# Mixer B's q, k and v of two head groups projected together, 512 columns wide, with roots taken on GpSimd

## The chip, the cores and the metric

The kernel runs on one core of one Trainium2 chip. The metric is the device time of one execution in microseconds (us). The core has a matmul engine (TensorE, PE), a vector engine (VectorE, DVE), an activation engine (ScalarE, ACT), a general engine (GpSimd, POOL) and a queue engine that only issues transfers here (SyncE, SP). Each works through its own instructions in order and waits for the others by semaphores.

## What is computed

The reference is a two-layer encoder trunk over 1024 tokens of width 1024. Layer 0 uses mixer A, a neighbourhood attention; layer 1 uses mixer B, which is what the change touches:

```python
def mixer_b(h, w_in, q_norm_g, k_norm_g, w_out):     # 16 query heads, 4 key/value heads, 64 wide
    proj = h @ w_in
    q, k, v, gate = jnp.split(proj, [MIX_WIDTH, MIX_WIDTH + kv_w, MIX_WIDTH + 2 * kv_w], axis=-1)
    q = rms_norm(q.reshape(b, s, B_Q_HEADS, HEAD_DIM), q_norm_g).transpose(0, 2, 1, 3)
    k = rms_norm(k.reshape(b, s, B_KV_HEADS, HEAD_DIM), k_norm_g).transpose(0, 2, 1, 3)
    v = v.reshape(b, s, B_KV_HEADS, HEAD_DIM).transpose(0, 2, 1, 3)
    q, k = _apply_axial_rope(q, tabs), _apply_axial_rope(k, tabs)
    ...
        sc = jnp.einsum('bkgqd,bksd->bkgqs', qb, k).astype(jnp.float32) * scale
        pr = jax.nn.softmax(sc, axis=-1).astype(v.dtype)
        return jnp.einsum('bkgqs,bksd->bkgqd', pr, v)
    ...
    return (o * jax.nn.silu(gate)) @ w_out
```

After each mixer come a residual sum, a per-layer gated embedding (the dense phase), and at the end a norm. Everything is in 32-bit floats.

## The kernel before

Tokens lie in 8 tiles of 128. The normalised input is kept transposed as a high and a low part, `HTh` and `HTl`, and each weight unit (128 x 1024) is split into a high part `wh` and a low part `wl`. A product is three matmuls, high x high, high x low, low x high (`split3`, through `mm`, so that nearly every matmul carries the line of `mm`). A weight unit is loaded by SyncE into `wstage`, ScalarE makes the high part and VectorE the low part (`Weights.pump`); the queue `q` sets the order of units, four slots hold units with slot number 1, and units with slot number 3 use a spare pair of the `KA`, `KB` buffers.

Mixer B has 4 groups of 4 query heads; a group shares one key/value head. The weights `bq` (256 columns of q for a group) and `bkv` (128 columns of k and 128 of v for a pair of groups) are applied by `q_items` and `kv_items`: for each token tile 8 x 3 matmuls of 256 columns into PSUM, cut into two pieces of 12 by `proj_N`, after which ScalarE copies the result out and squares it for the RMS norm, and two pieces of work later (`post.add(DR, rot)`) the sums and the rotation follow (`rope_in`). After every fourth tile `finish_norm` computes the inverse roots of the sums (`rsqrt_ops`: a bit-level first guess and three Newton steps, 11 small VectorE operations) and GpSimd multiplies them in (`scale_tile`). `k_stack` and `q_stack` then transpose k and q on TensorE into the layout of the scores. Gates (`gate_items`) are matmuls of 512 columns, in pieces of six.

The prologue, before attention starts, is written out by hand as the list `pre`: k, v of pair 0, q of group 0, the two halves of the k stack among the q pieces, the first query stack, the gate of pair 0 and the first scores. Between its first pieces it also transposes what is still pending from the dense phase (`pend`, `to_ht`): six pieces, of which the first two lie in buffers of the dense phase (`xn`). The first tiles of the prologue use the two score buffers of PSUM (`psS`).

Attention takes 32 steps per group: a step's scores (`f_S`), VectorE's minimum, ScalarE's exponential, transposes (`f_T`), and products with V. `mix` hands out the other, dense pieces between the steps in proportion: for group 0 the q of group 1 and a gate, for group 1 two gates, k, v of pair 1 and q of group 2, for group 2 two gates and q of group 3, for group 3 gate and embedding products. In the dense pieces of groups 0 to 2 the rotation runs on GpSimd.

Mixer A contains 32 transfers issued by GpSimd that add into DRAM (`weight_sums`); those are the only ones whose descriptors GpSimd writes, into a scratch at the start of SBUF that the program reserves (16 KB per partition unless it says otherwise).

## Time and profile before

| what | value |
|---|---|
| time, median of 3 runs | 1502.16 us (1500.39 to 1502.37) |
| profiled execution, its own time | 1500.79 us |
| its span in the trace | 1499.0 us |
| granted TensorE clock, mean | 0.998 of full speed |
| busy in the span: PE, DVE, ACT, POOL | 1478.6, 1069.6, 916.3, 445.2 us |
| mixer B's prologue | 694.6 to 757.2 us |
| groups 0, 1, 2 (by their first minimum on VectorE) | 757.2, 882.2, 1042.1 to 1178.2 us |

The span runs from the first to the last instruction in the trace; the own time has 1.8 us around it. Times inside the trace are counted from the span's start. "Busy" adds up the times in which an engine has an instruction running; matmuls overlap each other, so the rate of matmuls is read from their starts, not from their durations.

### The profile page before, as it was taken

How to read it: one execution, taken by the hardware profiler on the slowest of the kernel's cores; microseconds unless marked ns; L12 is line 12 of the kernel's file. 1: busy time of each engine (PE TensorE's matmuls, PEld its weight loads, DVE VectorE, ACT ScalarE, POOL GpSimd, SP SyncE). 2: the span in 40 equal slices, each digit the busy share in tenths (PEclk: the TensorE clock that was granted, in tenths of full speed). 3: DMA queues.
4: the chain of work that ended last, by engine and by line, in shares of the span. 5: the costliest groups of instructions: out<-in, count | busy, mean ns of one | idle time of the engine just before them, and what ended most of it. 6: DMA issues, size and time to landing. Idle time of an engine off the chain costs nothing.

```text
span 1499.0 us, 24720 instructions
## 1 busy us (share of the span) xinstructions
PE 1478.6 (99%) x8881; PEld 1302.8 (87%) x8881; DVE 1069.6 (71%) x2027; ACT 916.3 (61%) x1860; POOL 445.2 (30%) x637
## 2 busy tenths in 40 slices
PE   8999999999999999999999999999999999999997
PEld 8888988988988888888988999989999988888886
DVE  6666476477477598756887786777877787789845
ACT  6676476477477535433567776666767777745432
POOL 3355475387265200020322122443130300000000
PEclk9999999999999999999999999999999999999999
DMA  8424374283132862262210111111111122763223
GB/s 263 140 93 127 81 167 138 64 171 97 36 89 85 328 247 99 92 207 80 77 50 22 33 48 42 47 33 43 59 28 48 38 78 64 246 234 108 79 98 128
DMA packets 91466, 157.70 MB, mean 105 GB/s; under 512 B 18256, under 2 KB 54352, under 8 KB 90832
## 3 DMA queue, kind: packets, MB, share of 16 engines
q1 hardware_dynamic: 87344, 143.80, 28.9%
q0 software_dynamic: 2560, 8.39, 3.7%
q10 hardware_dynamic: 1440, 3.94, 0.8%
q8 instruction: 71, 1.16, 0.3%
q14 instruction: 51, 0.42, 0.1%
HBM read 125.56 MB, written 50.83 MB: 118 GB/s over the span
## 4 chain that ended last, share of the span: by engine, by line
PE 86%; DVE 6%; DMA 3%; ACT 2%; issue 1%; POOL 1%; SPq 1%; DVEq 0%; POOLq 0%; ACTq 0%
PE d L322 53%; PE s L322 11%; PE o L322 11%; PE t L1329 7%; PE t L821 2%; PE t L504 2%; DMA HTl<-yD0l 1%; DMA X<-in_x 1%; DVE wl L236 1%; PE t L322 1%; DVE PTl L1332 1%; DVE mn L1311 0%; PE t L1281 0%; DMA ppD<-G 0%; DVE xn L1674 0%
## 5 line engine op out<-in xcount | busy, mean ns | idle before, releaser
L322 PE MATMUL d<-wh,HTh 128*128 128x256 f32 (+1 forms) x1000 | 330.7, 335 | 0.3 <-ACT G L654 0.2
L322 PE MATMUL d<-wh,HTl 128*128 128x256 f32 (+1 forms) x1000 | 326.8, 331 | 0.5 <-DVE HTl L506 0.5
L322 PE MATMUL d<-wl,HTh 128*128 128x256 f32 (+1 forms) x1000 | 325.9, 330 | 0.6 <-DVE wl L1461 0.6
L1332 DVE TENSOR_TENSOR PTl<-t,PTh 128x512 fp32r<-128x512 f32 x256 | 164.6, 685 | 104.5 <-ACT PTh L1331 104.2
L322 PEld LDWEIGHTS d<-wl,HTh 128*128 128x128 f32 x1000 | 187.6, 189 | 20.2 <-DVE wl L1461 1.0
L322 PEld LDWEIGHTS d<-wh,HTh 128*128 128x128 f32 x1000 | 187.4, 189 | 19.9 <-ACT G L654 0.5
L322 PE MATMUL d<-HTh,wh 128*128 128x512 f32 x504 | 204.6, 406 | 0.0
L322 PEld LDWEIGHTS d<-wh,HTl 128*128 128x128 f32 x1000 | 187.5, 189 | 19.1 <-DVE HTl L506 0.9
L322 PE MATMUL d<-HTh,wl 128*128 128x512 f32 x504 | 198.1, 393 | 0.0
L322 PE MATMUL d<-HTl,wh 128*128 128x512 f32 x504 | 197.3, 392 | 0.0
L1317 ACT ACTIVATE P<-s,mn 128x1024 f32<-128x1024 f32 x128 | 142.9, 1117 | 47.9 <-DVE mn L1311 46.9
L1331 ACT ACTIVATE PTh<-t 128x512 fp32r<-128x512 f32 x256 | 139.4, 594 | 45.7 <-PE t L1329 45.2
L1311 DVE TENSOR_REDUCE mn<-s 128x1 f32<-128x1024 f32 x128 | 155.0, 1211 | 9.7 <-PE s L322 9.2
L831 POOL TENSOR_TENSOR PTh<-PTh,SIDE 128x256 fp32r<-128x256 f32 x96 | 81.4, 848 | 194.2 <-ACT PTh L826 194.1
L1329 PE MATMUL t<-ident,P 128*128 128x128 f32 x1024 | 134.9, 273 | 2.6 <-DVE PTl L1332 2.0
L322 PE MATMUL s<-KA,QS 128*128 128x512 f32 (+2 forms) x384 | 134.0, 403 | 0.0
L1329 PEld LDWEIGHTS t<-ident,P 128*128 128x128 f32 x1024 | 115.3, 140 | 12.9 <-DVE PTl L1332 7.1
L322 PE MATMUL s<-KB,QS 128*128 128x512 f32 (+2 forms) x384 | 121.5, 370 | 0.0
L322 PE MATMUL o<-PTl,V 128*128 128x256 f32 (+2 forms) x672 | 120.2, 290 | 1.1 <-DVE PTl L1332 0.6
L322 PE MATMUL o<-PTh,V 128*128 128x256 f32 (+2 forms) x672 | 118.3, 287 | 2.6 <-POOL PTh L831 1.3
L236 DVE TENSOR_TENSOR wl<-wstage,wh 128x1024 fp32r<-128x1024 f32 x79 | 98.1, 1243 | 29.3 <-ACT wh L231 29.0
L322 PEld LDWEIGHTS d<-HTh,wl 128*128 128x128 f32 x504 | 94.6, 188 | 21.6
(272 smaller groups left out, 2860.9 us busy)
## 6 DMA issues: line engine op xcount, KB each, us to landing
wstage<-in_wts SPq DMA_DIRECT2D x88, 512.0 KB
pp<-ppD SPq DMA_DIRECT2D x32, 256.0 KB
X<-in_x SPq DMA_DIRECT2D x15, 512.0 KB
rb<-rD SPq DMA_DIRECT2D x58, 128.0 KB
ppD<-th SPq DMA_DIRECT2D x20, 256.0 KB
tD0t<-in_wts SPq DMA_DIRECT2D x16, 256.0 KB
tD1t<-in_wts SPq DMA_DIRECT2D x16, 256.0 KB
xD<-X SPq DMA_DIRECT2D x8, 512.0 KB
```

The source lines that it names most:

```text
L236: eng.tensor_tensor(lo[:, c:c + n], s[:, c:c + n], hi[:, c:c + n], ALU.subtract)
L322: pe.matmul(ps, a, b, start=first, stop=last, skip_group_check=True)
L504: pe.transpose(ps[:, k], xn[:, (4 * c + k) * 128:(4 * c + k + 1) * 128], ident)
L821: pe.transpose(ps[:, i], sp[:, c * 128:(c + 1) * 128], ident)
L831: pool.tensor_tensor(pt[:, 3 * j - 1:3 * j + 4:4], pt[:, f1:f1 + 1].to_broadcast([128, 2, 128]), SIDE[:, :2], ALU.mult)
L1311: dve.tensor_reduce(mn, ps, axis=AX.X, op=ALU.min)
L1317: act.activation(p, ps, AF.Exp, bias=mn, scale=-1.0, accum_out=RS[h, hf][:, t:t + 1])
L1329: pe.transpose(ps[:, i], p[:, k * 128:(k + 1) * 128], ident)
L1331: act.activation(PTh[:, ks, c], ps, AF.Copy)
L1332: dve.tensor_tensor(PTl[:, ks, c], ps, PTh[:, ks, c], ALU.subtract)
```

## The change

The weight layout gets units `bqkv`: for group 0 with pair 0, and for group 1 with pair 1, the 256 columns of q and the 128 of k and 128 of v stand side by side, so that four units replace two of `bq` and two of `bkv`. `qkv_items` replaces `kv_items` and the first two uses of `q_items`: 8 x 3 matmuls of 512 columns for each tile, in two pieces of 12. ScalarE copies all 512 columns out and squares 384 of them. q of group 1 and k, v of pair 1 are computed together (`second`): the first two tiles at the end of the prologue, the other six beside group 0's attention; group 1 keeps the stacks of the second pair, two gates and q of group 2. The gates move: group 0 has gate 1, group 1 gates 2 and 3, group 2 gates 4 and 5, group 3 gates 6 and 7. The prologue becomes: eight wide tiles, with one half of the k stack after the sixth and the first query stack after the seventh, the gate of pair 0 (its weight in the spare `KA`, `KB` pair), the other half of the k stack after six of that gate's eight pieces, then the first two tiles of the second projection among the first scores. Pending transposes are taken before every piece from the second on, not before every other one from the third on.

Outside the prologue the roots are computed by one VectorE operation, GpSimd's power with exponent -0.5 (in columns of 16), and one Newton step of three VectorE operations; in the prologue they stay as they were, and k is scaled by VectorE there, q by GpSimd. The buffers `qtp`, `vp` and `tab` get more copies, and the scratch for software DMA is 2 KB instead of 16 KB.

```diff
@@ lay_out
-    for i in range(4):
+    for i in range(2, 4):
         put([("bq", i, 0), ("bq", i, 1)], bq[:, i * 256:(i + 1) * 256], 4)
     for i in range(2):
         s = slice(i * 128, (i + 1) * 128)
-        put([("bkv", i, 0), ("bkv", i, 1)], np.concatenate([bk[:, s], bv[:, s]], axis=1), 4)
+        put([("bqkv", i, u) for u in range(4)],
+            np.concatenate([bq[:, i * 256:(i + 1) * 256], bk[:, s], bv[:, s]], axis=1), 2)
@@ order of the weight units
-    q += [(("bkv", 0, 0), 1), (("bkv", 0, 1), 1), (("bq", 0, 0), 1), (("bq", 0, 1), 1), (("bg", 0), 1)]
-    for gi in range(4):
-        if gi > 0:
-            q.append((("bg", 2 * gi), 1))
-        if gi == 1:
-            q += [(("bkv", 1, u), 1) for u in range(2)]
+    for i in range(2):
+        q += [(("bqkv", i, u), 1) for u in range(4)] + [(("bg", i), 3)]
+    for gi in range(1, 4):
+        q.append((("bg", 2 * gi), 1))
         if gi < 3:
             q += [(("bq", gi + 1, u), 1) for u in range(2)]
         q.append((("bg", 2 * gi + 1), 1))
@@ proj_N
-            def end(k1=k1):
+            def end(k0=k0, k1=k1):
+                if release:
+                    WQ.done(*[u for u in release if k0 <= (keys.index(u) + 1) * per - 1 < k1])
                 if k1 == nk:
-                    if release:
-                        WQ.done(*release)
                     leave(lambda: evac(st["ps"]))
@@ mixer_b
-            qtp = es.enter_context(tc.tile_pool(name="qtp", bufs=3))
-            vp = es.enter_context(tc.tile_pool(name="vp", bufs=3))
+            qtp = es.enter_context(tc.tile_pool(name="qtp", bufs=5))
+            vp = es.enter_context(tc.tile_pool(name="vp", bufs=4))
...
-                tab = sb.tile([128, 2, 64], F32, name="tab", bufs=2)
+                tab = sb.tile([128, 2, 64], F32, name="tab", bufs=4)
@@ finish_norm
+                if pro[0]:
+                    ops = [lambda: dve.tensor_scalar(ss, ss, 0.5 / HD, 0.5 * EPS, op0=ALU.mult, op1=ALU.add)]
+                    ops += rsqrt_ops(ss, ss, wk)
+                    for i in range(2):
+                        post.add(1 + i, lambda i=i: [f() for f in ops[6 * i:6 * i + 6]])
+                    for raw, rs in tiles:
+                        post.add(2, lambda raw=raw, rs=rs: scale_tile(raw, rs, dve if rs.shape[1] == 2 else pool))
+                    return
+                y, a = wk[:, 0:n], wk[:, n:2 * n]
+
+                def power():
+                    dve.tensor_scalar(ss, ss, 4.0 / HD, 4.0 * EPS, op0=ALU.mult, op1=ALU.add)
+                    for c in range(0, n, 16):
+                        w = slice(c, min(c + 16, n))
+                        pool.tensor_tensor(y[:, w], ss[:, w], mhalf[:, :w.stop - c], ALU.pow)
+
+                def newton():
+                    dve.tensor_tensor(a, y, y, ALU.mult)
+                    dve.scalar_tensor_tensor(a, a, -1.0, ss, op0=ALU.mult, op1=ALU.mult)
+                    dve.scalar_tensor_tensor(ss, a, 3.0, y, op0=ALU.add, op1=ALU.mult)
+                post.add(DR, power)
+                post.add(DR + NP - 1, newton)
+                for i, (raw, rs) in enumerate(tiles):
+                    post.add(DR + NP + i, lambda raw=raw, rs=rs: scale_tile(raw, rs))
@@ qkv_items, in place of kv_items
+            def qkv_items(i, eng):
+                keys = [("bqkv", i, u) for u in range(4)]
...
+                    def evac(ps, t=t):
...
+                        raw = sb.tile([128, 512], F32, name="th")
+                        act.activation(raw, ps, AF.Copy)
+                        red = sumsq(raw[:, :384], 6, ss[:, t])
...
+                        def rot():
+                            red()
+                            rope_in(kr, raw[:, 256:384], tabk, eng)
+                            rope_in(qt, raw[:, :256], tabq, eng)
+                            for v, c in vs:
+                                eng.tensor_tensor(v[:, 64:], c, v[:, :64], ALU.subtract)
+                        post.add(1 if pro[0] else DR, rot)
...
+                    items += proj_N(keys, t, 512, alloc, evac, release=keys if t == NT - 1 else (), kstep=4)
@@ the prologue
-            pre = kv[:-2] + qi[:6] + kv[-2:-1] + qi[6:10] + kv[-1:] + qi[10:14]
-            fill = qi[14:] + [d for hf in range(2) for d in gate_items("bg", 0, hf, dalloc, sb, gg)]
-            pre += [glue(lambda: q_stack(0, 0))] + fill[:5]
-            pre += [glue(lambda: f_S(*steps[0]))] + fill[5:6] + [glue(lambda: f_E(*steps[0]))] + fill[6:7]
-            pre += [glue(lambda: f_S(*steps[1]))] + fill[7:]
+            first, second = qkv_items(0, dve), qkv_items(1, pool)
+            ks, gf = stacks(0), gates(0)
+            pre = first[:12] + ks[:1] + first[12:14] + [glue(lambda: q_stack(0, 0))] + first[14:]
+            pre += gf[:6] + ks[1:] + gf[6:] + second[:2]
+            pre += [glue(lambda: f_S(*steps[0]))] + second[2:3] + [glue(lambda: f_E(*steps[0]))]
+            pre += [glue(lambda: f_S(*steps[1]))] + second[3:4]
             for i, d in enumerate(pre):
-                if i >= 2 and i % 2 == 0 and pend:
+                if i >= 1 and pend:
                     to_ht(psT, *pend.pop(0))
@@ dense pieces of the groups
-                if g > 0:
-                    dense += left
-                if g < 3:
-                    qi = q_items(g + 1, pool)
-                    kv = kv_items(1, pool) if g == 1 else [None, None]
-                    dense += kv[:-2] + qi[:KS] + [k for k in kv[-2:-1] if k] + qi[KS:8] + [k for k in kv[-1:] if k] + gates(2 * g + 1) + qi[8:]
-                    left = gates(2 * g + 2)
+                if g == 0:
+                    gd = gates(1)
+                    n = len(gd) // 2
+                    dense += second[4:8] + gd[:n] + second[8:] + gd[n:]
...
+                else:
+                    gd = gates(2 * g)
+                    n = len(gd) // 2
+                    qi = q_items(g + 1, pool)
+                    ks = stacks(1) if g == 1 else []
+                    dense += gd[:n] + ks[:1] + gd[n:] + qi[:KS] + ks[1:] + qi[KS:8] + gates(2 * g + 1) + qi[8:]
@@ kernel
-    nc = bacc.Bacc("TRN2", target_bir_lowering=False, num_devices=1)
+    nc = bacc.Bacc("TRN2", target_bir_lowering=False, num_devices=1, dynamic_dma_scratch_size=2048)
```

What the change moves is shown at three places. First ScalarE at the start of mixer B, where the last copies of the transposed input (`HTh<-t`, from `to_ht`) stand among the copies of the first projection tiles out of PSUM (`th<-s`), before the change:

```order
L505 ACTIVATE HTh_75<-t_7468 128x512
L1834 ACTIVATE wstage_7476,sq_6706<-X7_6048 128x512
L1249 ACTIVATE th_7557<-s_7524 128x256
L1157 ACTIVATE t1_7559<-th_7557 128x128
L1255 ACTIVATE V_7550<-th_7557 128x64
L1255 ACTIVATE V_7553<-th_7557 128x64
L505 ACTIVATE HTh_75<-t_7563 128x512
L1249 ACTIVATE th_7605<-s_7572 128x256
```

And the same place with the change:

```order
L1863 ACTIVATE wstage_7476,sq_6706<-X7_6048 128x512
L504 ACTIVATE HTh_75<-t_7539 128x512
L1269 ACTIVATE th_7563<-s_7526 128x512
L1156 ACTIVATE t1_7565<-th_7563 128x384
L1275 ACTIVATE V_7559<-th_7563 128x64
L1275 ACTIVATE V_7560<-th_7563 128x64
L504 ACTIVATE HTh_75<-t_7582 128x512
L504 ACTIVATE HTh_75<-t_7606 128x512
L1269 ACTIVATE th_7625<-s_7593 128x512
```

One copy of transposed input has moved ahead of the first tile, and two instead of one stand between the first two tiles; the copy and the squares are wider.

Second VectorE in the prologue, after the last tile whose k the second half of the k stack transposes: the end of the roots (`ss`, `wk`) and what follows, with `wl1` the low half of a weight unit, before the change:

```order
L339 TENSOR_TENSOR wk_7912<-wk_7912 128x8
L340 TENSOR_TENSOR wk_7912<-wk_7912,ss_7556 128x8
L341 SCALAR_TENSOR_TENSOR ss_7556<-wk_7912 128x8
L1158 TENSOR_REDUCE ss_7963<-t1_7965 128x4
L1145 TENSOR_TENSOR t2_7992<-qt_7962,tab_7916 128x8x16 x2
L1146 TENSOR_TENSOR qt_7962<-qt_7962,tab_7916 128x256
L1148 TENSOR_TENSOR qt_7962<-qt_7962,t2_7992 128x256
```

And with the change:

```order
L338 TENSOR_TENSOR wk_8006<-wk_8006 128x24
L339 TENSOR_TENSOR wk_8006<-wk_8006,ss_7561 128x24
L340 SCALAR_TENSOR_TENSOR ss_7561<-wk_8006 128x24
L1193 TENSOR_TENSOR qt_7558<-qt_7558,ss_7561 128x128 x4
L627 SCALAR_TENSOR_TENSOR G_8074<-th_8073,G_8074 128x512
L237 TENSOR_TENSOR wl1_8092<-wstage_8063,wh1_8091 128x1024
L237 TENSOR_TENSOR wl1_8103<-wstage_8065,wh1_8102 128x1024
L1241 TENSOR_TENSOR KB_7887<-th_8099,KA_7886 64x512
```

The roots of k and q are now one set of 24 columns, VectorE scales k itself (`qt_7558` holds k), and the rotations of q no longer follow behind the k roots but stand before them, tile by tile.

Third GpSimd from the same place on, before the change:

```order
L1179 TENSOR_TENSOR qt_7549<-qt_7549,ss_7556 128x128 x8
L1227 COPY KA_7551<-KA_7551 64x512
L1228 COPY KB_7552<-KB_7552 64x512
L1227 COPY KA_7554<-KA_7554 64x512
L1179 TENSOR_TENSOR qt_7962<-qt_7962,ss_7963 128x256 x4
L1228 COPY KB_7555<-KB_7555 64x512
```

And with the change, from the scaling of q of tiles 4 to 7:

```order
L1193 TENSOR_TENSOR qt_7814<-qt_7814,ss_7561 128x256 x4
L1246 COPY KA_7886<-KA_7886 64x512
L1247 COPY KB_7887<-KB_7887 64x512
L1246 COPY KA_7888<-KA_7888 64x512
L1144 TENSOR_TENSOR t2_8175<-th_8167,tab_8130 128x4x16 x2
L1145 TENSOR_TENSOR qt_8162<-th_8167,tab_8130 128x128
L1147 TENSOR_TENSOR qt_8162<-qt_8162,t2_8175 128x128
L1144 TENSOR_TENSOR t2_8180<-th_8167,tab_8128 128x8x16 x2
L1145 TENSOR_TENSOR qt_8166<-th_8167,tab_8128 128x256
L1147 TENSOR_TENSOR qt_8166<-qt_8166,t2_8180 128x256
L1283 TENSOR_TENSOR V_8163<-th_8167,V_8163 128x64
L1283 TENSOR_TENSOR V_8164<-th_8167,V_8164 128x64
```

GpSimd no longer scales k in the prologue, and the rotation of the second projection's first tile, q, k and v from one copy `th`, now follows the copies of k directly.

## Rows read from the trace of the kernel before

**Rows 1.** The page's busy times: us, share of the span, instructions.
```profile
PE 1478.6 (99%) x8881; PEld 1302.8 (87%) x8881; DVE 1069.6 (71%) x2027; ACT 916.3 (61%) x1860; POOL 445.2 (30%) x637
```

**Rows 2.** Windows of prologue and groups: busy us by engine, then clock, DMA share, GB/s.
```profile
694.60:757.20 62.60, 61.41 (x467) 58.83 (x468) 52.00 (x165) 28.51 (x72) 12.61 (x21) 1.00 0.21 68
757.20:882.20 125.00, 124.68 (x882) 113.68 (x881) 97.03 (x147) 92.86 (x171) 29.65 (x43) 1.00 0.11 34
882.20:1042.10 159.90, 158.55 (x1132) 146.81 (x1131) 117.04 (x202) 109.05 (x216) 62.86 (x112) 1.00 0.15 44
1042.10:1178.20 136.10, 136.10 (x956) 126.00 (x955) 105.30 (x166) 97.59 (x179) 34.02 (x48) 1.00 0.14 41
```

**Rows 3.** Timeline of PE, 256 columns, first and last of 43: start, us.
```profile
716.07 0.28 PE L322 MATMUL s<-wh,HTh 128*128 128x256 f32 x1
...
721.11 0.28 PE L322 MATMUL s<-wh,HTh 128*128 128x256 f32 x1
```

**Rows 4.** Timeline of PE, 512 columns, first and last of 57.
```profile
544.64 0.39 PE L322 MATMUL d<-wh,HTh 128*128 128x512 f32 x1
...
557.43 0.39 PE L322 MATMUL d<-wh,HTl 128*128 128x512 f32 x1
```

**Rows 5.** Chain that ended last, merged: start, us; prologue piece and attention piece.
```profile
705.94 2.88 PE s L322 x24
...
805.01 1.39 PE d L322 x6
```

**Rows 6.** Chain at the start of the prologue, 701 to 703.
```profile
701.05 0.45 PE t L504 x4
```

**Rows 7.** Timeline of PE there; idle time and releaser in brackets.
```profile
702.36 0.39 PE L322 MATMUL s<-wh,HTh 128*128 128x256 f32 x1 [0.88 <-ACT th L1249]
```

**Rows 8.** Chain before the first query stack, 738 to 746.
```profile
741.20 2.07 POOL qt L1179 x3
```

**Rows 9.** Waits of PE, 694 to 1180: us in total, times, longest.
```profile
PE t L1281 <- POOL qt L1179: 0.3, 1, 0.3
```

**Rows 10.** Timeline of DVE in the prologue.
```profile
704.07 0.28 DVE L1158 TENSOR_REDUCE ss<-t 128x2 f32<-128x128 f32 x1
...
705.56 0.69 DVE L506 TENSOR_TENSOR HTl<-t,HTh 128x512 fp32r<-128x512 f32 x1
...
731.34 0.41 DVE L1158 TENSOR_REDUCE ss<-t 128x4 f32<-128x256 f32 x1
...
732.98 0.41 DVE L1158 TENSOR_REDUCE ss<-t 128x4 f32<-128x256 f32 x1
...
737.77 0.17 DVE L1165 TENSOR_SCALAR ss<-ss 128x16 f32<-128x16 f32 x1
...
740.07 0.69 DVE L1222 TENSOR_TENSOR KB<-th,KA 64x512 fp32r<-64x512 f32 x1
...
744.48 0.40 DVE L1158 TENSOR_REDUCE ss<-t 128x4 f32<-128x256 f32 x1
...
747.09 0.69 DVE L1222 TENSOR_TENSOR KB<-th,KA 64x512 fp32r<-64x512 f32 x1
...
749.76 1.41 DVE L1291 TENSOR_TENSOR QS<-th,QS 64x512 fp32r<-64x512 f32 x2
751.19 1.23 DVE L236 TENSOR_TENSOR wl<-wstage,wh 128x1024 fp32r<-128x1024 f32 x1
```

**Rows 11.** Lines of ACT by shape, 695 to 1320: busy, mean ns, idle before.
```profile
L623 ACT ACTIVATE G<-d 128x512 f32<-128x512 f32 x15 | 9.0, 599 | 13.5 <-PE d L322 13.5
```

**Rows 12.** Lines of POOL by shape, whole span.
```profile
L1145 POOL TENSOR_TENSOR t<-qt,tab 128x128 f32<-128x128 f32 x48 | 22.5, 490 | 164.2 <-ACT qt L1193 50.4 <-PE t L1329 46.4 <-issue 40.7
...
L346 POOL TENSOR_TENSOR wkn<-sa,mhalf 128x4 f32<-128x4 f32 x2 | 2.0, 1010 | 20.8 <-DVE sa L1659 20.8
```

**Rows 13.** Line 680, software DMA: ns min/median/max, first and last start.
```profile
L680 POOL DMA_DIRECT2D tD0t<-tD0t x8: 780/1200/1967, 185.3 to 207.0; - x8
...
DMA to landing us min/median/max: 3.7/5.0/6.9
```

More of the change, by code (lines that the diff above doesn't have):

```diff
@@ L64, in weight_units @@
     names += [("ag", p) for p in range(8)]
-    for g in range(4):
+    for i in range(2):
+        names += [("bqkv", i, u) for u in range(4)]
+    for g in range(2, 4):
         names += [("bq", g, u) for u in range(2)]
-    for i in range(2):
-        names += [("bkv", i, u) for u in range(2)]
     names += [("bg", p) for p in range(8)]
@@ L173, in trunk @@
     make_identity(nc, ident)
-    mhalf = glob.tile([128, 4], F32, name="mhalf")
+    mhalf = glob.tile([128, 16], F32, name="mhalf")
     pool.memset(mhalf, -0.5)
@@ L1124, in mixer_b @@
             gg, ylive = {}, {}
-            KA, KB, V, QT, QST, P, RS, OP = {}, {}, {}, {}, {}, {}, {}, {}
+            KA, KB, KR, V, QT, QST, P, RS, OP = {}, {}, {}, {}, {}, {}, {}, {}, {}
             later = Later()
@@ L1155, in sumsq @@
             def sumsq(ps, nh, ss):
-                t1 = sb.tile([128, 256], F32, name="t1", bufs=1)[:, :nh * 64]
+                t1 = sb.tile([128, 384], F32, name="t1", bufs=1)[:, :nh * 64]
                 act.activation(t1, ps, AF.Square)
@@ L1164, in finish_norm @@
                 wk = sb.tile([128, 96], F32, name="wk", bufs=1)
-                ops = [lambda: dve.tensor_scalar(ss, ss, 0.5 / HD, 0.5 * EPS, op0=ALU.mult, op1=ALU.add)]
-                ops += rsqrt_ops(ss, ss, wk)
-                per = -(-len(ops) // (2 if pro[0] else NP))
-                at = DR
-                for i in range(0, len(ops), per):
-                    post.add(at, lambda i=i: [f() for f in ops[i:i + per]])
-                    at += 1
-                for raw, rs in tiles:
-                    post.add(at, lambda raw=raw, rs=rs: scale_tile(raw, rs))
-                    at += 0 if pro[0] else 1
@@ L1176, in scale_tile @@
-            def scale_tile(raw, rs):
+                n = ss.shape[1]
+                if pro[0]:
+                    ops = [lambda: dve.tensor_scalar(ss, ss, 0.5 / HD, 0.5 * EPS, op0=ALU.mult, op1=ALU.add)]
+                    ops += rsqrt_ops(ss, ss, wk)
+                    for i in range(2):
+                        post.add(1 + i, lambda i=i: [f() for f in ops[6 * i:6 * i + 6]])
+                    for raw, rs in tiles:
+                        post.add(2, lambda raw=raw, rs=rs: scale_tile(raw, rs, dve if rs.shape[1] == 2 else pool))
+                    return
@@ L1208, in q_items, with k_stack @@
                 return items
-            def k_stack(i, raw, hf):
+            def k_stack(i, hf):
+                raw = KR[i]
+                if hf == 0:
+                    for j in range(2):
+                        KA[2 * i + j] = kp.tile([128, 1024], F32R, name="KA")
+                        KB[2 * i + j] = kp.tile([128, 1024], F32R, name="KB")
                 ps = psT.tile([128, 4, 128], F32, name="t")
@@ L1352, in mixer_b, with gates, stacks @@
             pro[0] = True
-            kv, qi = kv_items(0, dve), q_items(0, dve)
+            WQ.cap[3] = 1
             glue = lambda f: (f, 0.0)
-            pre = kv[:-2] + qi[:6] + kv[-2:-1] + qi[6:10] + kv[-1:] + qi[10:14]
-            fill = qi[14:] + [d for hf in range(2) for d in gate_items("bg", 0, hf, dalloc, sb, gg)]
-            pre += [glue(lambda: q_stack(0, 0))] + fill[:5]
-            pre += [glue(lambda: f_S(*steps[0]))] + fill[5:6] + [glue(lambda: f_E(*steps[0]))] + fill[6:7]
-            pre += [glue(lambda: f_S(*steps[1]))] + fill[7:]
+            def gates(p):
+                return [i for hf in range(2) for i in gate_items("bg", p, hf, dalloc, sb, gg)]
+            def stacks(i):
+                return [(lambda hf=hf: k_stack(i, hf), 450.0) for hf in range(2)]
+            first, second = qkv_items(0, dve), qkv_items(1, pool)
[4 more added lines that the diff above has]
+            pre += [glue(lambda: f_S(*steps[1]))] + second[3:4]
             for i, d in enumerate(pre):
-                if i >= 2 and i % 2 == 0 and pend:
+                if i >= 1 and pend:
                     to_ht(psT, *pend.pop(0))
```

45 lines of the change are left out of this document (18 added, 27 removed).

## The prediction

> **What bounds the kernel now.** I read the busy shares first: TensorE is busy for 99% of the span, VectorE for 71%, GpSimd for 30% [rows 1]. Then I cut mixer B into its prologue and its first three head groups. The reader is to see in the windows that TensorE is idle for only 1.19, 0.32, 1.35 and 0.00 us of them, at a granted clock of 1.00, that is at the 2.4 GHz level, throughout [rows 2]. So nearly all that can be won is TensorE's own work, and nearly all that can be lost is a new wait of TensorE. Neither the 71% nor the 30% limits anything by itself, but in the prologue VectorE is busy for 52.00 of 62.60 us, and there a late VectorE can hold TensorE.
>
> "Busy" hides the rate at which matmuls follow each other, so I read starts. 256-column matmuls follow at 0.120 us (43 starts, 716.07 to 721.11: 5.04 / 42) [rows 3]. 512-column ones follow at 0.228 us (57 starts, 544.64 to 557.43: 12.79 / 56) [rows 4]. Two narrow ones cost 0.240, a wide one 0.228, for the same columns.
>
> **The change, part by part.**
>
> *Wide instead of narrow matmuls.* The q projections of groups 0 and 1 and the k, v projections of both pairs are 4 x 192 = 768 matmuls of 256 columns; they become 384 of 512. I count in pieces of 12 wide ones for 24 narrow: 32 pieces, 20 in the prologue and 12 among group 0's attention steps. 24 narrow take 2.88 [rows 5]. 12 wide take 12 x 0.228 = 2.74 in a quiet stretch; between attention steps six took 1.39, so 12 take 2.78 [rows 5]. 20 x 0.14 + 12 x 0.10 = **4.0 us won**. Ends: all at 0.10, 3.2; all at 0.14, 4.5.
>
> The Trainium skill, "TensorE: Matmul & The Clock Gate", section "Back-to-back issue gap", gives N/2.4 ns plus 2.5 ns between isolated matmuls at the full clock. By that, 24 narrow and 12 wide take 2.62 and 2.59 us, and the 32 pieces would win an estimated 1.0 us, not 4.0: a rule that speaks against the change. The rows show 120 and 228 ns where it has 109 and 216, so each instruction here costs some 13 ns beside its columns, and I go by the rows.
>
> *The entry.* Before, TensorE stood for 0.88 at 702.36, for ScalarE's first copy out of PSUM [rows 7]. That copy stood on ScalarE behind the second of the two transposed pieces that still lay in the earlier stage's buffers (701.05, ended 701.50) [rows 6], while both score buffers were full. Now these two pieces stand before the second and third half tile instead of before the third and fifth, and filling the second buffer takes 2 x 2.74 us instead of 2.88. The copy is therefore done some 5 us before TensorE wants the buffer: **0.9 won** (ends 0 and 0.9).
>
> *The first query stack.* GpSimd scaled three tiles of q from 741.20 to 743.27 [rows 8], and TensorE waited 0.3 for it [rows 9]. Now tile 3 ends three wide tiles ahead of that stack (3 x 2 x 2.74 = 16 us), against some 10 us of work: 1.5, 3.1, 2.3 and 1.2 as worked out for the next step, and 4 x 0.69 of GpSimd's scales [rows 8]: **0.3 won** (ends 0 and 0.3).
>
> *The second k stack.* This is the new wait. Before, the k roots were ready long before q was projected, and nothing else stood behind them. Now k of tiles 4 to 7 is ready only after the last wide tile, and six gate pieces (6 x 1.39 = 8.3) lie between that tile and the transposes that need it. In that time: ScalarE's copy of 512 columns 0.60 [rows 11] and the squares, which I put at the same, with 0.3 of hand-overs, 1.5; VectorE's k part 1.49 (704.07 to 705.56) and q part 1.64 (731.34 to 732.98), together 3.1; eleven root operations 2.3 (737.77 to 740.07); a weight's low half between them 1.2; four k scales at an estimated 0.3 (the seven operations of the k part take 0.21 each), 1.2 [rows 10]. Sum 9.3. VectorE also comes about 0.5 late to that tile, because the stack's query halves (1.41) and another low half (1.23) stand in front [rows 10]. 9.3 + 0.5 - 8.3 = **1.5 lost**. Below: 0, if hand-overs and scales are shorter. Above: with GpSimd working beside it the q part took 2.61 (744.48 to 747.09) instead of 1.64 [rows 10]; if all 7.8 us of VectorE's chain stretch by a quarter, 3.5. Behind the waiting transposes stand all of TensorE's queue, so the wait counts in full.
>
> The Trainium skill, "SBUF — State Buffer", section "Who interferes with whom", says that VectorE with two SBUF inputs and a GpSimd instruction that reads SBUF exclude each other. By that rule, the trace agrees: 2.61 against 1.64. The upper end is the row's with or without it; GpSimd has only query scales and three short copies to do there.
>
> *Attention of groups 0 and 1.* The dense work beside their 32 steps was 34 us (16 x 1.44 for q and 8 x 1.39 for a gate) and 68 (32 x 1.44 and 16 x 1.39). It becomes 44 (12 x 2.78 and 8 x 1.39) and 45 (16 x 1.44 and 16 x 1.39), and 45 is what group 2 has. Group 2 has no idle time, groups 0 and 1 have 1.67 together [rows 2]. The stacks of the second pair stay in group 1, with their waits. I take **0.5 won**; ends 1.7 won, 1.5 lost, if GpSimd's longer rotations hold the two shared scratch tiles. GpSimd has ten operations of about 0.5 for a tile [rows 12], 5 us, and two pieces of dense work with the attention steps between them are longer than that; only at the start do two tiles follow closely, with copies of k between them.
>
> *Costed at nothing.* The roots by power: GpSimd's power took 1.01 for 4 columns [rows 12] and now has up to 24, at most 6 us; all of it lies in groups 0 to 2, where the stacks that need it stand a gate projection or more behind; if that cover went, those 6 us a set would show. Root work taken from VectorE (8 small operations a set): not on the path in attention. The four weight units are again the first four in the queue, so they are split where four were split before. The second pair's units are freed one by one at tile 7 and have some ten pieces of work until they are wanted. The table loads go from one to two per tile on SyncE's queue, each with two tiles of lead by four buffers; behind them there stand weight loads and row sums, which are fetched earlier than they are used by more than that. The smaller scratch: the transfers that use it are 32, issued by GpSimd in mixer A, at most two in flight at the times shown [rows 13].
>
> **Sum.** -4.0 - 0.9 - 0.3 + 1.5 - 0.5 = -4.2. The profiled execution took 1500.79 (span 1499.0 and 1.8 outside), so 1496.6 in its terms. The median of the runs, 1502.16, is 1.37 above it; on that footing **1498.0**. All good ends give -7.4, all bad ends +1.8.
>
> **Rivals.**
> - *No new wait, and even groups.* The k stack comes in time and groups 0 and 1 run like group 2: another 1.5 and 1.2 won, 1495.3. For it: group 2's windows. Against: VectorE's sum above. Chance 0.15.
> - *The new wait eats the gain.* Wide matmuls win only 3.2, the k stack waits 3.5 and attention gives nothing: -3.2 - 0.9 - 0.3 + 3.5 = -0.9, 1501.3. For it: VectorE's stretched rows. Chance 0.24.
> - *It does not do what it says:* a wide matmul takes as long as two narrow ones. Then -0.2, 1502.0. Rows 3 and 4 speak against it. Chance 0.03.
> - *Slower: the scratch throttles GpSimd.* The second eight transfers of a layer are issued 3.1 us apart (185.3 to 207.0, seven intervals) and land in 5.0 [rows 13]. If the small scratch held fewer than two, each would wait 1.9 for the one before: 16 x 1.9 = 30 us of GpSimd time in mixer A, where it edits the score tiles that TensorE reads. If a third of that came through, +10: 1508. It decides as soon as one transfer fills the scratch; nothing in the trace shows its size. Chance 0.08.
>
> The forecast itself has 0.50, and its own range is 1496 to 1499.5.
>
> **How the numbers follow.** 0.2% is 3.0 us, about what a measurement of this kernel can tell from no change: faster means under 1499.2, slower over 1505.2. Of the forecast's 0.50, 0.43 lies below 1499.2; with the first rival 0.58 faster. 0.07, 0.24 and 0.03 make 0.34 the same; 0.08 slower. The range 1494.5 to 1502.5 takes in everything but the slower rival and the outer edges of the others.
>
> **What would show it.** The 512-column projection matmuls start 0.228 apart in the prologue and no more than 0.232 between steps. No wait stands before the third tile's first matmul. TensorE's largest idle time in the prologue stands before the second k stack's transposes, 1 to 2 us, ended by VectorE's k scale. Groups 0 and 1 have about equal lengths, near 135 us. GpSimd's transfers take as long as before. I am wrong if the wide matmuls keep 0.24, if that wait is over 3.5, or if TensorE waits for GpSimd in group 0.

## The result, and the profile after

The changed kernel is slower: 1505.53 us in the median of 11 runs (1503.74 to 1508.0) against 1502.16 of the kernel before, ratio 1.0021 (95% interval 1.0013 to 1.0029). The forecast was 1498.0, and its range ended at 1502.5. The profiled execution took 1508.0, 7.2 more than that of before (1500.79).

The busy times of the page, as in [rows 1]:

```profile
PE 1478.2 (98%) x8497; PEld 1284.1 (85%) x8497; DVE 1060.0 (70%) x1933; ACT 911.4 (61%) x1828; POOL 461.2 (31%) x637
```

TensorE has 384 matmuls less and the same busy time, since a wide one counts longer. The loss is in idle time. The windows of prologue and groups 0, 1, 2, cut at each group's first minimum as in [rows 2]:

```profile
694.60:767.30 72.70, 68.95 (x312) 55.77 (x311) 52.85 (x148) 30.63 (x65) 11.54 (x19) 0.98 0.24 77
767.30:912.80 145.50, 139.11 (x846) 119.83 (x845) 102.26 (x143) 96.28 (x182) 63.53 (x105) 1.00 0.13 38
912.80:1051.50 138.70, 137.07 (x952) 125.20 (x951) 101.77 (x149) 99.43 (x182) 37.63 (x49) 1.00 0.11 31
1051.50:1186.20 134.70, 134.70 (x946) 124.97 (x945) 104.99 (x153) 98.70 (x180) 39.51 (x50) 1.00 0.15 46
```

The lengths can't be set against those of before one by one, since work has moved between the stages; the idle times can. They were 1.19, 0.32, 1.35 and 0.00; they are 3.75, 6.39, 1.63 and 0.00, so 8.9 more. And the granted clock of the prologue is 0.98 instead of 1.00. Who was waited for, first in the prologue, then in group 0 (us in total, times, longest; `PTh` and `PTl` are the high and low parts of the transposed probabilities `P`):

```profile
PE t L1232 <- DVE qt L1193: 2.2, 4, 1.4
PE t L503 <- DVE HTl L505: 1.3, 1, 1.3
...
PE t L1350 <- DVE PTl L1353: 2.8, 3, 1.3
PE o L321 <- ACT PTh L1352: 1.6, 6, 0.3
PE t L1302 <- DVE PTl L1353: 1.3, 1, 1.3
PE t L1350 <- ACT P L1338: 0.6, 3, 0.2
```

The first row is the second k stack, where the forecast had put its new wait. TensorE's timeline there (idle time and releaser in brackets):

```profile
752.11 0.39 PE L321 MATMUL o<-HTh,KB 128*128 128x512 f32 x1
753.93 0.30 PE L1232 MATMUL t<-ident,qt 128*128 128x128 f32 x1 [1.43 <-DVE qt L1193]
754.46 0.33 PE L1232 MATMUL t<-ident,qt 128*128 128x128 f32 x1 [0.23 <-DVE qt L1193]
755.08 0.39 PE L1232 MATMUL t<-ident,qt 128*128 128x128 f32 x1 [0.29 <-DVE qt L1193]
755.70 0.47 PE L1232 MATMUL t<-ident,qt 128*128 128x128 f32 x1 [0.23 <-DVE qt L1193]
755.83 0.77 PE L321 MATMUL o<-HTh,KA 128*128 128x512 f32 x1
756.40 0.63 PE L321 MATMUL o<-HTl,KA 128*128 128x512 f32 x1
...
758.53 0.44 PE L321 MATMUL o<-HTh,KA 128*128 128x512 f32 x1
758.81 0.39 PE L321 MATMUL o<-HTl,KA 128*128 128x512 f32 x1
```

Two things are to be seen. All four transposes wait, each for its own k scale. By starts the wait is 3.0: 755.70 - 752.11 is 3.59, of which a wide matmul (0.23) and three transposes (0.11 each) are work. And behind it 512-column matmuls follow at 0.43 instead of 0.23 until 758.5: 755.83 to 758.81 is 2.98 for seven, which take 1.59 at full rate, another 1.4 lost. The windows of 2 us there show the same as a mean granted clock of 0.55 and 0.59, that is for the most part the 1.2 GHz level:

```profile
753.00:755.00 2.00, 0.63 (x2) 1.00 0.73 215
755.00:757.00 2.00, 1.69 (x5) 0.55 0.34 113
757.00:759.00 2.00, 2.00 (x7) 0.59 0.16 23
759.00:761.00 2.00, 2.00 (x10) 1.00 0.98 279
```

What was forecast as won is there. The chain shows 72 wide matmuls of the prologue (six pieces) and one piece of group 0:

```profile
716.13 16.38 PE s L321 x72
...
857.20 2.73 PE d L321 x12
```

16.38 / 72 is 0.2275, and 2.73 / 12 the same.

Up to the end of group 2 the profiled execution is 8.0 later (1186.2 against 1178.2). That is about 8.9 of idle time, 1.4 of the slow clock and 2 for what the brackets leave out (the wait at 753.93 is 1.43 there and 1.59 by starts; some 14 gaps more at 0.15), less 4.5 of narrow matmuls saved (below), and 0.6 by which this execution came later to the projection's first matmul (695.16 against 694.60). Together 8.4. The medians differ by less, 3 to 5 us: the profiled execution is the slowest of its 11 (1508.0 against a median of 1505.53), and that of before lies 1.4 under its median. Another execution of the changed kernel, below, has no wait at the pending transposes; which waits the executions without a trace had, nothing shows.

### The profile page after: what moved, and what is told of

Its sections match the earlier page's. It is cut to its first block, busy times and chain, and to the rows that moved or that the text cites. A ratio compares the mean times of both kernels' runs of the same rounds, so it can differ in the third digit from the quotient of the medians.

```text
span 1506.1 us, 23817 instructions
## 1 busy us (share of the span) xinstructions
PE 1478.2 (98%) x8497; PEld 1284.1 (85%) x8497; DVE 1060.0 (70%) x1933; ACT 911.4 (61%) x1828; POOL 461.2 (31%) x637
## 4 chain that ended last, share of the span: by engine, by line
PE 86%; DVE 5%; ACT 4%; issue 2%; DMA 1%; POOL 1%; SPq 0%; DVEq 0%; ACTq 0%; POOLq 0%
PE d L321 53%; PE s L321 11%; PE o L321 10%; PE t L1350 6%; PE t L820 2%; PE t L503 1%; PE t L321 1%; DVE PTl L1353 1%; ACT PTh L1352 1%; DVE mn L1332 1%; ACT wh L232 1%; ACT P L1338 1%; DMA wstage<-in_wts 0%; DMA rb<-rD 0%; PE t L1302 0%
## 5 line engine op out<-in xcount | busy, mean ns | idle before, releaser
L321 PE MATMUL d<-wh,HTh 128*128 128x512 f32 (+1 forms) x896 | 305.9, 346 | 1.1 <-ACT HTh L504 0.8
L321 PE MATMUL d<-wh,HTl 128*128 128x512 f32 (+1 forms) x896 | 303.7, 343 | 0.5 <-DVE HTl L505 0.5
L321 PE MATMUL d<-wl,HTh 128*128 128x512 f32 (+1 forms) x896 | 302.8, 342 | 0.2 <-DVE wl L1490 0.2
L321 PE MATMUL d<-HTh,wh 128*128 128x512 f32 x480 | 194.1, 404 | 0.0
L321 PE MATMUL d<-HTh,wl 128*128 128x512 f32 x480 | 188.4, 392 | 0.0
L321 PE MATMUL d<-HTl,wh 128*128 128x512 f32 x480 | 187.9, 391 | 0.0
L321 PEld LDWEIGHTS d<-wh,HTh 128*128 128x128 f32 x896 | 167.5, 189 | 21.9 <-ACT HTh L504 1.1
L321 PEld LDWEIGHTS d<-wl,HTh 128*128 128x128 f32 x896 | 167.6, 189 | 21.6 <-DVE wl L1490 0.6
L321 PEld LDWEIGHTS d<-wh,HTl 128*128 128x128 f32 x896 | 167.5, 189 | 21.3 <-DVE HTl L505 0.9
L321 PEld LDWEIGHTS o<-PTh,V 128*128 128x128 f32 x672 | 98.1, 190 | 15.0 <-ACT PTh L1352 7.2
```

The source lines that it names most:

```text
L321: pe.matmul(ps, a, b, start=first, stop=last, skip_group_check=True)
```

## The experiments

Five rounds each, beside the kernel before on the same chip. "Group 0" is the time from its first minimum to group 1's, "prologue" the time from the projection's first matmul to there, both from the run's trace. That matmul starts between 693.1 and 697.0 us, so times counted from the span's start can't be compared between traces to better than that.

| run | median us | ratio to before (95%) | prologue | group 0 |
|---|---|---|---|---|
| before | 1502.16 | | 62.6 | 125.0 |
| changed | 1505.53 | 1.0021 (1.0013 to 1.0029) | 72.1 | 145.6 |
| e_again | 1506.53 | 1.0032 (1.0021 to 1.0044) | 70.9 | 145.6 |
| e_split | 1509.48 | 1.0051 (1.0038 to 1.0064) | 72.8 | 147.6 |
| e_kstack | 1502.08 | 1.0000 (0.9992 to 1.0009) | 66.6 | 145.8 |
| e_pend | 1509.13 | 1.0048 (1.0034 to 1.0062) | 74.1 | 145.6 |
| e_scratch | 1502.25 | 1.0005 (0.9997 to 1.0014) | 62.5 | 125.0 |
| e_six | 1500.58 | 0.9992 (0.9982 to 1.0002) | 71.9 | 140.8 |
| e_roots | 1506.48 | 1.0029 (1.0020 to 1.0039) | 70.4 | 145.7 |
| e_all1 | 1504.54 | 1.0021 (1.0013 to 1.0030) | 74.4 | 142.2 |
| e_ks6 | 1497.42 | 0.9969 (0.9957 to 0.9980) | 66.6 | 140.8 |
| e_ks6_roots | 1497.71 | 0.9973 (0.9964 to 0.9982) | 66.5 | 139.7 |
| e_ks6_late | 1493.12 | 0.9941 (0.9929 to 0.9954) | 67.9 | 136.9 |
| e_sq | 1505.39 | 1.0025 (1.0014 to 1.0035) | 70.9 | 144.5 |

Ahead of the first minimum lies the same work in the changed kernel and all its variants; in the kernel before it is other work.

**e_again.** No edit.

> The changed kernel once more, for a second trace of it and for a median on the same chip as its variants. Theory: TensorE waits about 3.0 us in all at the second half of the k stack (the first transpose 1.6, the next three 0.4 to 0.5 each), 1.5 at the last pending transposes, and about 6 in group 0's attention; the time is 1505.5 (ratio 1.002). The fall of the granted clock behind the k stack (0.98 in the first trace) comes in some executions only, so this one may be 1.5 to 2 shorter than the first profiled execution. Rival: the first profiled execution (1508.0) was an odd one and these waits are not there in another: then idle time in the prologue and group 0 together is under 5 us.

Group 0 takes 145.6 again; its waits are no accident. The k stack waits 1.62, 0.42, 0.51 and 0.51 by starts, and the slow clock is there again. The wait at the pending transposes is not: there the first table of the rotation landed by 703.76, where VectorE began its rotation, and in the first trace only by 705.87 (9.3 and 10.7 us after the projection's first matmul), with the low half of a pending piece behind that rotation. The profiled execution is 1.8 shorter than the first, as expected, but for this reason and not for the clock's. Of the ten traces that take the pending transposes as changed, two have this wait (1.47 and 1.26 by starts).

**e_split.** Wide matmuls cut in two:

```diff
+                    if keys[0][0] == "bqkv":
+                        for u in range(2):
...
+                            split3(st["ps"][:, o], HTh[:, t, k, :], HTl[:, t, k, :], wh[:, c2], wl[:, c2], k == 0, k == nk - 1)
+                        continue
```

> Every 512-column projection matmul is issued as two of 256 columns; layout, pieces and order stay as changed. Theory (the wide matmuls do win what was forecast, and waits eat it): 4.0 us slower than the changed kernel, 1509.5 (1508.7 to 1510.0), ratio to before 1.0048. Rival (a wide matmul takes as long as two narrow ones): 1505.5. Between: if the longer pieces give late engines more cover, part of the 4.0 comes back in group 0's waits, 1507 to 1508.

Two sums run in turns in one PSUM buffer here and are not those of the reference; only the time is read. The chain has 144 narrow matmuls where 72 wide ones stood, and a piece of group 0:

```profile
713.80 17.27 PE s L321 x144
...
772.37 2.88 PE d L321 x24
```

17.27 / 6 is 2.88 for a piece, against 2.73: 0.15, and group 0, which holds 14 of the 32 pieces behind its first minimum, is 2.0 longer, 0.14 each. 32 x 0.14 is 4.5. Up to the end of group 0 its trace is 3.9 longer than e_again's, with a wait at the k stack that is 0.3 shorter. The median is 2.9 higher; the intervals of the two ratios leave room for 4.5. That a wide matmul takes as long as two narrow ones is excluded.

**e_kstack.** The k stack behind all eight gate pieces:

```diff
-            pre += gf[:6] + ks[1:] + gf[6:] + second[:2]
+            pre += gf + ks[1:] + second[:2]
```

> The second half of the k stack stands behind all eight gate pieces of the prologue instead of six: 2.8 us more of TensorE work in front of it. Theory: the first transpose finds its k scaled, the waits of about 3.4 us there fall to about 0.6 and the clock does not fall: 1505.5 - 2.8 = 1502.7, and up to 1.6 less where the clock had fallen. Rival: the wait only moves to the first scores, which need the stack's copies by VectorE and GpSimd: 1505.5, with the idle time in front of the first scores.

It is 4.4 faster than e_again on the same chip, and equal to the kernel before. In the trace one gap of 0.32 is left at the stack, the first scores don't wait, and the clock is 1.00 throughout the prologue:

```profile
694.60:760.20 65.60, 65.44 (x307) 53.88 (x306) 50.57 (x145) 28.82 (x62) 10.48 (x18) 1.00 0.26 84
```

2.8 us of cover removed 4.4 us of e_again's prologue (70.9 to 66.6): the wait of 3.0 but for 0.3, and the fall of the clock behind it. The forecast of this run, 2.8 and up to 1.6 more where the clock had fallen, came true with both.

**e_pend.** Pending transposes as in the kernel before:

```diff
-                if i >= 1 and pend:
+                if i >= 2 and i % 2 == 0 and pend:
```

> The pending transposes are taken before every other piece from the third on, as in the kernel before; all else as changed. Theory: the 1.5 us wait for VectorE's low half, which stands behind a rotation that waits for its table, goes, and at most the earlier kernel's wait of 0.9 for ScalarE's first copy comes in its place: 1505.5 - 1.0 = 1504.5 (1504.0 to 1505.0). Rival: with later transposes the buffers that hold weights come free later, and the weights of the projection are late: 1507 or more, with TensorE waiting for a weight.

Slower by 2.6 than e_again: the theory fell, the rival held. The waits in its prologue:

```profile
PE d L321 <- ACT KA L232: 1.8, 1, 1.8
PE s L321 <- ACT th L1269: 0.8, 1, 0.8
...
SPq L215 <- PE t L503: 8.0, 1, 8.0
```

The second row is the old wait for ScalarE's first copy, 0.98 by starts, so the changed order does remove what the forecast said. The first is a weight: the gate's high part in `KA` is late. The third is SyncE's own queue: four of the pending pieces lie in the two `wstage` buffers that weights are loaded into, and the loads (`L215`) wait for their transposes, 8.0 here against 2.7 in e_again. Behind the late weight the granted clock fell too, to 0.56 and 0.58 in the windows from 749 to 753. I had taken the earlier transposes for a cause of loss; they are a gain.

**e_scratch.** The kernel before with the small scratch:

```diff
-    nc = bacc.Bacc("TRN2", target_bir_lowering=False, num_devices=1)
+    nc = bacc.Bacc("TRN2", target_bir_lowering=False, num_devices=1, dynamic_dma_scratch_size=2048)
```

> The kernel before with nothing but the scratch of 2 KB. Theory: no change, 1502.2, ratio 1.000 within 0.001, GpSimd's 32 transfers take 0.8 to 1.4 us each as before. Rival: the scratch throttles GpSimd: transfers of over 2 us and 1504 or more.

No change. The second eight transfers of a layer, as in [rows 13]:

```profile
L680 POOL DMA_DIRECT2D tD0t<-tD0t x8: 785/1209/1971, 185.9 to 207.7; - x8
```

**e_six.** Group 0's wide tiles in pieces of six matmuls:

```diff
-                    items += proj_N(keys, t, 512, alloc, evac, release=keys if t == NT - 1 else (), kstep=4)
+                    items += proj_N(keys, t, 512, alloc, evac, release=keys if t == NT - 1 else (), kstep=2 if i and t > 1 else 4)
...
-                    dense += second[4:8] + gd[:n] + second[8:] + gd[n:]
+                    dense += second[4:12] + gd[:n] + second[12:] + gd[n:]
```

> The changed kernel with group 0's six wide tiles cut into four pieces of six matmuls (1.39 us) instead of two of 12. Theory: waits in group 0 stand at steps that have no dense piece in front of their products, where ScalarE's copy of a tile (1.5 us with the squares) stands in front of the copies of the transposes; with a piece at nearly every step these nine waits of 0.35 to 0.45 go: 1505.5 - 3.2 = 1502.3. Rival: ScalarE, VectorE and GpSimd have too much to do in group 0 and the same waits stand elsewhere: 1505.5.

The second hunk keeps the order, since two tiles are now eight pieces. Group 0 is 4.8 shorter, the time 5.9 lower than e_again's (measured at two times, with medians of the kernel before that differ by 0.15). The changed kernel has thirteen gaps of over 0.3 by starts in group 0, 8.5 in all: nine of 0.35 to 0.45 behind ScalarE (3.7) and four behind VectorE's `PTl` (1.37, 0.49, 1.51, 1.45). They become two, one of 3.5 at group 0's end and one of 0.35. The profiled execution is the slowest of its 12 (1505.0), with the longest slow stretch behind the k stack: the clock reads 0.50 in three windows on end. It fell again behind the wait of 3.5 (0.50 from 901 to 907), and reads 0.994 over the whole execution.

```profile
755.00:757.00 2.00, 1.86 (x6) 1.46 (x6) 2.00 (x3) 1.24 (x2) 0.67 (x2) 0.50 0.06 17
757.00:759.00 2.00, 2.00 (x7) 1.52 (x6) 2.00 (x3) 0.82 (x2) 1.05 (x1) 0.50 0.30 72
759.00:761.00 2.00, 2.00 (x6) 1.59 (x5) 0.57 (x1) 0.12 (x1) 0.64 (x2) 0.50 0.93 289
```

**e_sq.** Pieces of 12; ScalarE's squares and V copies one item later:

```diff
+                        def rest():
+                            red.append(sumsq(raw[:, :384], 6, ss[:, t]))
...
+                        if pro[0]:
+                            rest()
+                        else:
+                            post.add(1, rest)
```

> The changed kernel, pieces of 12 and all else as changed, but in attention ScalarE's squares and V copies of a projection tile (0.53 and 0.39 us) come one item later, behind the copies of the transposed probabilities instead of in front. Theory A (what is late at a step without a dense piece is ScalarE's copy of the probabilities, held by the wide tile's work in front of it): the nine waits of 0.35 to 0.45 go, group 0 from 145.6 to 142.3, 1506.5 - 3.3 = 1503.2. Theory B (it is the length of the pieces alone, TensorE has nothing between the transposes and the products): the waits stay, 1506.5.

Between the two theories. A step without a dense piece looks like this in the changed kernel, first ScalarE, then TensorE:

```profile
797.66 0.60 ACT L1269 ACTIVATE th<-d 128x512 f32<-128x512 f32 x1 [1.68 <-PE d L321]
798.29 0.53 ACT L1156 ACTIVATE t<-th 128x384 f32<-128x384 f32 x1
798.72 0.39 ACT L1275 ACTIVATE V<-th 128x64 fp32r<-128x64 f32 x2
799.01 1.06 ACT L1352 ACTIVATE PTh<-t 128x512 fp32r<-128x512 f32 x2
...
799.64 1.22 PE L321 MATMUL o<-PTh,V 128*128 128x256 f32 x8 [0.28 <-ACT PTh L1352]
...
802.01 1.09 PE L1350 MATMUL t<-ident,P 128*128 128x128 f32 x8 [0.19 <-ACT P L1338]
```

The tile's 1.5 us on ScalarE stand in front of the transposes' copies, on which the products wait (0.45 by starts), and then in front of the exponential, on which the next transposes wait (0.35). With the squares behind the copies the six waits of the products are gone, but those of the transposes grow to 0.71 to 0.77: the exponential comes later. Group 0 gains 1.1 of the 3.3. So ScalarE's burst at a wide tile's end is what is late, and moving it within the same gap pays little; a dense piece at every step pays all of it.

**e_roots.** The earlier roots in attention:

```diff
-                post.add(DR, power)
-                post.add(DR + NP - 1, newton)
+                ops = [lambda: dve.tensor_scalar(ss, ss, 0.5 / HD, 0.5 * EPS, op0=ALU.mult, op1=ALU.add)]
+                ops += rsqrt_ops(ss, ss, wk)
+                for i in range(0, 12, 2):
+                    post.add(DR + i // 2, lambda i=i: [f() for f in ops[i:i + 2]])
...
-                    post.add(DR + NP + i, lambda raw=raw, rs=rs: scale_tile(raw, rs))
+                    post.add(DR + 6 + i, lambda raw=raw, rs=rs: scale_tile(raw, rs))
```

> The changed kernel with the earlier way of the roots (three Newton steps on VectorE, no power on GpSimd) in attention too. Theory: the waits behind the second set's power in group 0 (0.49, 1.51 and 1.45 us, where VectorE's Newton step waits 1.43 for a power of 5.5 us and low halves take 3.87 instead of 2.46) go or fall under 1 in all: 1505.5 - 2.5 = 1503.0. Rival: these waits come from the query scales and low halves that collide, with or without the power: 1505.5; or VectorE's extra operations (18 more of 0.2 for two sets) delay it more: 1506.5.

No gain, as the rival has it: gaps of 0.49, 1.51 and 1.45 at group 0's end become 1.97, 0.70 and 0.29, and one of 1.37 in its middle becomes 2.13. This run alone would have cleared the power. It stood beside other late work at the same place: the weight units loaded where the last tile frees the old ones, whose low halves VectorE makes there, slowly beside GpSimd. The changed kernel, GpSimd and then VectorE:

```profile
891.38 5.51 POOL L1179 TENSOR_TENSOR wk<-ss,mhalf 128x16 f32<-128x16 f32 x2
...
896.92 0.18 DVE L1182 TENSOR_TENSOR wk<-wk 128x24 f32<-128x24 f32 x1 [1.43 <-POOL wk L1179]
...
897.46 1.28 DVE L1353 TENSOR_TENSOR PTl<-t,PTh 128x512 fp32r<-128x512 f32 x2
...
899.79 3.87 DVE L237 TENSOR_TENSOR wl<-wstage,wh 128x1024 fp32r<-128x1024 f32 x2
903.59 1.27 DVE L1353 TENSOR_TENSOR PTl<-t,PTh 128x512 fp32r<-128x512 f32 x2
```

VectorE waits for the power, the `PTl` copies wait behind VectorE's wait, and TensorE waits for the copies.

**e_all1.** The edits of e_kstack, e_pend and e_six together.

> The changed kernel with the k stack two pieces later, the pending transposes as before and group 0's tiles in pieces of six together. Theory: -2.8 - 1.0 - 3.2, 1498.5 (1497.5 to 1500.5), ratio 0.9976. Rival: as the prologue gets shorter, the same late engines make TensorE wait a little further on, and no more than half comes through: 1502.

1504.54: e_pend's late weights are in it, 3.9 of waits for weights in its prologue. The next three runs leave that edit out.

**e_ks6.** The edits of e_kstack and e_six.

> The changed kernel with the k stack two pieces later and group 0's tiles in pieces of six; the pending transposes as changed. Theory: both gains add, since they lie in different stages: 1506.5 - 4.4 (prologue, waits and the fallen clock) - 4.8 (group 0's length, 145.6 to 140.8) + 1.0 (group 1, 138.7 to 139.7) = 1498.3, ratio 0.998 (0.997 to 0.9985). Rival: they overlap, and it is no faster than pieces of six alone, 1500.6.

1497.42, 0.31% faster than the kernel before; the two gains all but add (4.4 and 5.9 off e_again's 1506.53 would be 1496.1). One wait of TensorE is left in group 0, 3.3 in the list of waits (3.47 by starts), put down to VectorE. VectorE, then GpSimd, then the clock in a window behind the wait:

```profile
890.91 1.26 DVE L1182 TENSOR_TENSOR wk<-wk 128x24 f32<-128x24 f32 x1 [2.02 <-POOL wk L1179]
892.21 0.18 DVE L1183 SCALAR_TENSOR_TENSOR wk<-wk,ss 128x24 f32<-128x24 f32 x1
892.43 1.13 DVE L1184 SCALAR_TENSOR_TENSOR ss<-wk 128x24 f32<-128x24 f32 x1
...
890.84 1.30 POOL L610 TENSOR_TENSOR Y<-Y,G 128x512 f32<-128x512 f32 x1
892.21 1.30 POOL L611 TENSOR_TENSOR Y<-Y,rb 128x512 f32<-128x512 f32 x1
...
897.00:899.00 2.00, 2.00 (x12) 0.50 0.00 0
```

VectorE waits 2.0 for the power, and two of its three Newton steps then end only as a GpSimd operation ends, 2.0 more. The next minimum and the sum that TensorE waits for stand behind them.

**e_ks6_roots.** The same with e_roots' edit.

> The same with the earlier way of the roots in attention. With pieces of six one wait of 3.5 us is left in group 0, at its end, where VectorE's Newton step waits 2.0 for GpSimd's power of 24 columns (5.5) and its steps take 1.27 and 1.13 instead of 0.18 beside GpSimd. Theory: without the power this wait goes: 1498.3 - 3.0 = 1495.3. Rival, as in the run with the earlier roots alone: another late operation, the low halves of the four units that come free at the last tile, takes its place: 1498.3.

1497.71, no gain: the wait is 2.96 instead, behind VectorE's eleven root operations and two low halves (one of 2.32) at the same place.

**e_ks6_late.** The power kept, its Newton step and the scales five items later:

```diff
-                post.add(DR + NP - 1, newton)
+                post.add(DR + NP + 4, newton)
...
-                    post.add(DR + NP + i, lambda raw=raw, rs=rs: scale_tile(raw, rs))
+                    post.add(DR + NP + 5 + i, lambda raw=raw, rs=rs: scale_tile(raw, rs))
```

> The same as the first of these, with the power, but VectorE's Newton step and the scales five items later, so that the power is done when VectorE comes to it. Theory: the wait of 3.5 us goes without giving up the power: 1495.5. Rival: GpSimd stays late and its scales collide with VectorE further on: 1498.3.

1493.12, 4.3 below e_ks6 and 0.59% below the kernel before. VectorE now finds the power done, without idle time in front of it, and each step takes 0.17 or 0.18 (the third too):

```profile
895.36 0.17 DVE L1182 TENSOR_TENSOR wk<-wk 128x24 f32<-128x24 f32 x1
895.56 0.18 DVE L1183 SCALAR_TENSOR_TENSOR wk<-wk,ss 128x24 f32<-128x24 f32 x1
```

Group 0 is left with 0.8 of idle time (136.9 long, 136.10 busy), in an execution that had the 1.26 of the pending transposes too. Its granted clock is 1.00 there, where e_ks6's fell to 0.50 behind its wait; so the 4.3 hold the wait and the slow clock behind it.

## Why the prediction was wrong, point by point

*Wide instead of narrow matmuls, 4.0 won: right, 4.5 by the matmuls' starts; the medians of e_split and e_again differ by 2.9.* 12 wide ones take 2.73 in attention too, not 2.78. The Trainium skill's 2.5 ns beside the columns ("TensorE: Matmul & The Clock Gate", section "Back-to-back issue gap") would have made it an estimated 1.0; the starts in e_split decide for the rows.

*The entry, 0.9 won: right in eight of ten traces*, and e_pend brings the 0.98 back. In the other two a first table that landed 1.2 and 1.5 us later after the projection's first matmul than e_again's costs 1.3 and 1.5, just ahead of the third tile, where the forecast had said that no wait stands. The prediction costed the doubled table loads at nothing, by their lead in buffers; the first tile's has no such lead.

*The first query stack, 0.3 won: right.* No wait stands there.

*The second k stack, 1.5 lost: right in place and releaser, too small.* The wait is 3.0, inside the 3.5 of the upper end. Two terms of the sum were short. ScalarE's copy of the last tile was taken to follow it at once, but began 1.8 after the tile's end (the next matmul starts at 744.17), behind the query stack's halves and a weight's high part. And four k scales were put at 1.2 and took 2.15 beside GpSimd's scales of q:

```profile
744.99 1.06 ACT L232 ACTIVATE wh<-wstage 128x1024 fp32r<-128x1024 f32 x1
745.96 0.58 ACT L1269 ACTIVATE th<-s 128x512 f32<-128x512 f32 x1
...
753.49 2.15 DVE L1193 TENSOR_TENSOR qt<-qt,ss 128x128 f32<-128x128 f32 x4
...
753.60 2.51 POOL L1193 TENSOR_TENSOR qt<-qt,ss 128x256 f32<-128x256 f32 x4 [9.25 <-DVE ss L340]
```

The rest (rotation 2.9, roots and a low half 3.4) came out within 0.3 of the sum. What had no term at all is the clock that falls behind this wait: 1.4 in the first trace. With it the k stack costs 4.4, and e_kstack's 4.4 on the median agrees.

*Attention of groups 0 and 1, 0.5 won (1.7 won to 1.5 lost): this is the step that failed.* It said that group 0 gets 44 us of dense work, about group 2's 45, and so group 2's zero idle time. Group 0 waits for 6.39. Groups 0 and 1 together are idle for 8.0 instead of 1.67, 6.4 lost where 0.5 won was forecast, far outside the worst end; and they are 145.6 and 138.7 long, not both near 135. The amount of work was right; what decides is how it is cut and what comes with each piece. Group 2 has 32 pieces of 1.4 for its 32 steps. Group 0's six tiles came in 12 pieces of 2.73 beside 8 of 1.39, 20 in all, so that a dozen steps have none, and each tile ends in 1.5 us of ScalarE's work. e_six shows the size of it: group 0 is 4.8 shorter. None of the three marks of being wrong that the forecast named came up: wide matmuls took 0.2275, the k stack's wait is under 3.5, and in group 0 the list of waits names VectorE and ScalarE, with GpSimd only behind VectorE.

*Power roots, costed at nothing: wrong.* I named as cover the time until the stack needs the roots. What needs them first is the Newton step, and behind it in VectorE's queue stand the copies, minima and sums on which TensorE waits. It gave 24 columns "at most 6 us", and two operations take 4.5 in the first set of group 0 and 5.5 in the second. e_ks6 to e_ks6_late shows the cost, 4.3 with the slow clock behind the wait. It is not the power alone but the place of the step that waits for it, since the old roots at that place are no better (e_roots, e_ks6_roots).

*The second pair's units "have some ten pieces of work until they are wanted": true for TensorE*, which never waits for them in group 0, but not free: the low halves of the units loaded in their place (3.87 for two) delay `PTl`.

*The scratch: right*, by e_scratch. Its rival, the one of a slower kernel, is excluded; the kernel is slower by other ways: a k stack that costs 4.4 where 1.5 stood in the sum, and waits in attention where a gain of 0.5 stood. The rival with the right place (the new wait eats the gain, 1501.3) had left attention at nothing too.

Not separated: how much the later Newton step alone gives in the kernel with pieces of 12; whether the later step or the later scales, which moved with it, give e_ks6_late its gain; how much of the 4.3 is the clock; and which execution gets its first table late, which no run here controls.

## What to carry to other kernels

When wider instructions make pieces of work fewer and longer, count the pieces against the steps that they fill, and look at what each piece leaves on the other engines: equal total work doesn't mean equal cover. An operation moved to an idle engine is hidden only if nothing that waits for it stands in a busy engine's queue ahead of critical work; place the waiting operation late, by the slowest case. When one edit alone shows no gain (e_roots), its place may hold several late things, and it is worth asking again once the others are gone.
